# Forming the rests of the first phase's weight blocks with an accumulating DMA

## Chip, cores and metric

One core of a Trainium2 chip runs the whole program. The metric is the device time of one execution in microseconds (us), the median of several runs. The engines named here are PE (TensorE, matmuls; PEld is its weight load), DVE (VectorE), ACT (ScalarE), POOL (GpSimd) and SP (SyncE, which only issues DMAs here). DMAs are issued by SP, ACT or POOL and run on 16 DMA engines that all of them share.

## The reference

One step of a hybrid decoder layer for 512 prompt tokens and 8 single-token samples, T = 520 columns in all. It begins with one wide projection of x and goes on with two recurrent branches, a merge, cross-attention and an MLP:

```python
p = x @ W['w_in'][l]                      # (T, 1024) x (1024, 7424): 58 blocks of 128 columns
p_rw = p[..., :N_SHIFT]                   # r, k, v and the low-rank codes: 26 blocks
o_rw, s_rw_l = _rwkv7_branch(p_rw, p_prev, s_rw[l], l, W)      # 16 heads, delta rule with decay
o_lru, h_l, conv_l = _rglru_branch(p[..., C_U:C_Y], p[..., C_Y:C_GATE], s_conv[l], s_h[l], l, W)
gates = jax.nn.sigmoid(p[..., C_GATE:].reshape(p.shape[:-1] + (2, D_MODEL)) + W['mix_gate_b'][l])
mix = (gates[..., 0, :] * o_rw + gates[..., 1, :] * o_lru) @ W['w_out_mix'][l]
x = _layer_norm(ALPHA * x + mix, W['ln1_g'][l], W['ln1_b'][l])
xa = _mem_attention(x, mem_k[l], mem_v[l], W['xa_wq'][l], W['xa_wo'][l])
x = _layer_norm(ALPHA * x + xa, W['ln2_g'][l], W['ln2_b'][l])
hdn = jnp.square(jax.nn.relu(x @ W['mlp_up'][l]))
x = _layer_norm(ALPHA * x + hdn @ W['mlp_down'][l], W['ln3_g'][l], W['ln3_b'][l])
```

All arrays are float32.

## The kernel before

**Split products.** A float32 product is made of three matmuls in the rounded format F32R: a weight block w is split into a rounded part h = round(w) and a rest l = w - h, x likewise, and `mm3` (L123) adds wh·xh, wh·xl and wl·xh, in this order, for each of the eight 128-row slices of the block. A unit of work is one block of 1024x128 weights: 48 matmuls, half of them over the first 256 columns of x, half over the other 264. So the rest of a block is first read by the third matmul of its unit.

**Units.** `unit` and `wunit` (L149, L152) append to the list `units`; `adv` (L171) runs the next one. Before it runs unit i it calls `prep(i + 1 + AHEAD)` with AHEAD = 2 (L155), and `prep` calls `split_w` (L89) for each block not yet prepared. So a block is loaded and split two units ahead of its use.

**The split (L89 to L99).** SP loads the block into `raw` (tag `wr`, 512 KB in rows of 512 bytes, two buffers), ACT casts it into `h` (tag `wh`, L95), and DVE subtracts: `l = raw - h` (tag `wl`, L98). `wh` and `wl` have three buffers each. The cast of block i+2 therefore waits until the matmuls of unit i-1 have read that buffer for the last time, and the load into a `raw` buffer waits until the subtraction that read it has ended.

**The first phase.** Its 58 units are the blocks of `w_in`: two low-rank codes (`u_code`), 24 of r, k, v (`u_rkv`), 16 of the RG-LRU branch (`u_L`), 16 of the gates (`u_G`). Their epilogues run on ACT and DVE (`shifted`, L441: L445, L446, L447), those of `u_G` on ACT, with stores from POOL (L576). Between the units run the stages of the RWKV-7 branch for four pairs J of head groups: E1, E2, E3 (elementwise, ACT and DVE), C1 (products within a chunk), C2 (a triangular solve of 30 dependent steps on DVE, L718 and L720, with units called in between as filling), the recurrent chain (`stage_chain`, L746: short matmuls with copies on ACT, L771, L806, and on DVE, L778, L794, between them, one step after every 13 to 16 other matmuls) and GN (normalization). After the first phase come the projections of the memory, of the branches, and so on; their blocks go through the same `split_w` or, in the MLP, through `need` (L1641).

**POOL** begins with the loads of the parameter rows (L291), then adds the parts of x and stores them (L1205, L1206; two buffers), and later makes small copies for the outputs (L533, L540, L564), scales `ar` (L678), clears tiles (L682, L714) and issues stores (L566, L576, L851). It takes its instructions in the order of its queue.

**What sets the order.** The program is written for a planner that puts each engine's instructions into an order by the place in the program and by when the inputs should be ready. `keep_in_program_order` pins an instruction behind those already written for its engine. Each engine then runs its own order and waits for semaphores.

Of the kernel before, what the change touches and what calls it, by code (L numbers as in the profile page):

```python
# [8 lines left out]
F32 = mybir.dt.float32  # L9
F32R = mybir.dt.float32r  # L10
AF = mybir.ActivationFunctionType
OP = mybir.AluOpType
# [24 lines left out]
def build(tc, d, dbg=None):  # L37
    nc = tc.nc
    ACT, DVE, POOL, SP = nc.scalar, nc.vector, nc.gpsimd, nc.sync
# [49 lines left out]
    def split_w(src, shape, pool):  # L89
        raws.append(raws.pop(0))  # L90
        raw = raws[-1].tile([128, *shape], F32, tag="wr", name="wr")
        SP.dma_start(out=raw, in_=src)
        h = pool.tile([128, *shape], F32R, tag="wh", name="wh")
        l = pool.tile([128, *shape], F32R, tag="wl", name="wl")
        a = ACT.copy(h, raw)  # L95
        if state["behind"]:
            tc.keep_in_program_order(a)
        DVE.tensor_tensor(l, raw, h.bitcast(F32), op=OP.subtract)  # L98
        return h, l  # L99


# [42 lines left out]

    AHEAD = 2
    units = []
    state = {"prep": 0, "run": 0, "later": [], "x": None, "half": 0, "behind": False}

    def unit(src, fn, shape=(KT, 128), extra=0):  # L149
        units.append([src, fn, shape, extra, None])  # L150
# [4 lines left out]
    def prep(n):  # L155
        while state["prep"] < min(n, len(units)):
            u = units[state["prep"]]
            u[4] = split_w(u[0], u[2], state["x"][u[3] - 1] if u[3] else wsp)
            state["prep"] += 1
# [11 lines left out]
    def adv(n=1):  # L171
        for _ in range(n):
            i = state["run"]
            if i >= len(units):
                return
            prep(i + 1 + AHEAD)
            u = units[i]
            state["run"] += 1
            u[1](u[4])
            u[4] = None  # L180
            flush(False)
# [309 lines left out]
    def u_rkv(q, j):  # L491
        def run(w):
            s, nm = j % 2, "rkv"[q]
            o = et(nm + str(s))
            shifted(mm_full(w, X), q * KT + j, o)
            pair.setdefault(j, {})[nm] = o
        wunit("w_in", q * D + j * 128, run)
# [633 lines left out]
    def u_kv(nm, i):  # L1131
        def run(w):
            p = mmps()[:, 0, 0:N_MEM]
            n = 0
            for k in range(KT):
                c = slice(k % 2 * N_MEM, (k % 2 + 1) * N_MEM)
                for a, b in ((w[0], mem["h"]), (w[0], mem["l"]), (w[1], mem["h"])):
                    PE.matmul(p, a[:, k], b[k // 2][:, c], start=n == 0, stop=n == 3 * KT - 1)
                    n += 1
            ft = (E.tile([128, 2, N_MEM], F32, tag="s1", name="ft", bufs=2) if i % 4 < 2 else  # L1140
                  E.tile([128, 2, N_MEM], F32, tag=("bk", "kp")[i % 2], name="ft"))
            ACT.copy(ft[:, 0], p)  # L1142
            if nm == "xa_wk":
                ACT.dma_start(out=kT_d[i], in_=ft[:, 0])

            def rows():
                pt = ps1()
                for m in range(2):
                    PE.transpose(pt[:, m * 128:(m + 1) * 128], ft[:, 0, m * 128:(m + 1) * 128], ident)
                ACT.copy(ft[:, 1], pt[:, 0:N_MEM])  # L1150
                tok = ft[:, 1].rearrange("p (m n) -> p m n", m=2)
                cs = slice(i * 128, (i + 1) * 128)
                ACT.dma_start(out=d["mem_k_p" if nm == "xa_wk" else "mem_v_p"][0, 0].rearrange(
                    "(m p) h e -> p m (h e)", p=128)[:, :, cs], in_=tok)
                if nm == "xa_wv":
                    ACT.dma_start(out=v_d.rearrange("m p n -> p m n")[:, :, cs], in_=tok)
            later(rows, 2)
        wunit(nm, i * 128, run)
# [16 lines left out]
    C2U = ("kGKGGrv", "GKGkrv", "kKrv")  # L1175
    CHU = ("LLVR", "LLRV", "LLRV")
    FILL = ((3, 4, 8, 18, 20, 21, 22), (3, 7, 9, 16, 28, 31), (3, 13, 23, 28))
    for J in range(3):
        j = 2 * J + 2
        for c in C2U[J] + CHU[J] + "GGG":  # L1180
            if c == "L":
# [4 lines left out]
            else:  # L1186
                u_rkv("rkv".index(c.lower()), 2 * J + 2 + c.isupper())
    CHU = [c.replace("L", "LL") for c in CHU]
    for i in range(KT):
        u_kv("xa_wk", i)  # L1190
    for i in range(4):
# [19 lines left out]
    for J in range(4):  # L1211
# [9 lines left out]
        if J < 3:  # L1221
# [3 lines left out]
            queue(stage_E1(J + 1))  # L1225
            n = len(CHU[J])
            adv(n - (2, 4, 4)[J])
# [620 lines left out]
    def more():  # L1848

        x = ExitStack()  # L1850
        state["x"][1] = x.enter_context(tc.tile_pool(name="wx2", bufs=2, reuse_waits="tile"))
        return x

    adv(KT)
    x = more()
# [29 lines left out]
    x = more()  # L1885
# [103 lines left out]
```

## Time and profile before

| | |
|---|---|
| three runs, us | 1382.88, 1374.3, 1370.4 (median 1374.3) |
| the profiled execution, us | 1374.86 |
| its span, first to last instruction, us | 1373.2 |
| mean granted clock of TensorE | 0.977 |
| busy: PE, DVE, ACT, POOL | 94%, 71%, 46%, 26% of the span |

The profile is of one execution. Its page gives the busy time of each engine, the span in 40 slices of 34.3 us with the busy share in tenths, the queues of the DMAs and the costliest groups of instructions. The trace behind it can be asked for stretches, groups, waits and instructions in order of time. Matmuls overlap, so their durations add up to more than PE's time. "idle before <-X" names what ended the wait before an instruction.

### The profile page before, as it was taken

How to read it: one execution, taken by the hardware profiler on the slowest of the kernel's cores; microseconds unless marked ns; L12 is line 12 of the kernel's file. 1: busy time of each engine (PE TensorE's matmuls, PEld its weight loads, DVE VectorE, ACT ScalarE, POOL GpSimd, SP SyncE). 2: the span in 40 equal slices, each digit the busy share in tenths (PEclk: the TensorE clock that was granted, in tenths of full speed). 3: DMA queues.
4: the chain of work that ended last, by engine and by line, in shares of the span. 5: the costliest groups of instructions: out<-in, count | busy, mean ns of one | idle time of the engine just before them, and what ended most of it. 6: DMA issues, size and time to landing. Idle time of an engine off the chain costs nothing. (4 is left out here: it accounts for less than half of the span.)

```text
span 1373.2 us, 27593 instructions
## 1 busy us (share of the span) xinstructions
PE 1287.6 (94%) x11098; PEld 1195.0 (87%) x11098; DVE 977.0 (71%) x1921; ACT 625.7 (46%) x1202; POOL 356.5 (26%) x415
## 2 busy tenths in 40 slices
PE   7997999999999999878899998989999999999996
PEld 7996998798879787777879998767999999999996
DVE  5578976798669777988954545665668677777755
ACT  4475376437653657542254334432454333333321
POOL 6312000200020012117413133262111444534312
PEclk9999999999999999989999999999999999999998
DMA  6422322231222123475549536684332333333311
GB/s 199 132 78 69 101 66 73 78 101 49 76 91 70 32 80 120 120 204 163 178 140 297 150 107 192 202 262 157 90 102 81 96 91 108 93 93 96 106 64 63
DMA packets 205973, 160.30 MB, mean 117 GB/s; under 512 B 12429, under 2 KB 190911, under 8 KB 205334
## 3 DMA queue, kind: packets, MB, share of 16 engines
q1 hardware_dynamic: 182502, 104.36, 26.0%
q0 software_dynamic: 14592, 47.80, 10.5%
q10 hardware_dynamic: 8752, 6.39, 1.5%
q8 instruction: 87, 1.43, 0.5%
q14 instruction: 40, 0.33, 0.1%
HBM read 137.11 MB, written 21.40 MB: 115 GB/s over the span
## 5 line engine op out<-in xcount | busy, mean ns | idle before, releaser
L47 PE MATMUL mm<-xH,wh 128*128 128x260 f32 (+2 forms) x1824 | 480.9, 292 | 6.3 <-ACT wh L95 2.1
L47 PE MATMUL mm<-xL,wh 128*128 128x256 f32 (+2 forms) x1824 | 473.2, 288 | 1.0 <-DVE ff L1817 1.0
L47 PE MATMUL mm<-xH,wl 128*128 128x264 f32 (+2 forms) x1568 | 453.1, 289 | 0.8 <-DVE wl L98 0.8
L47 PEld LDWEIGHTS mm<-xH,wh 128*128 128x128 f32 x1824 | 329.7, 191 | 16.7 <-issue 3.8
L47 PEld LDWEIGHTS mm<-xL,wh 128*128 128x128 f32 x1824 | 328.7, 190 | 7.8 <-issue 4.5
L47 PEld LDWEIGHTS mm<-xH,wl 128*128 128x128 f32 x1568 | 298.2, 190 | 7.2 <-issue 3.8
L95 ACT CAST wh<-wr 128x1024 fp32r<-128x1024 f32 x120 | 125.1, 1053 | 169.4 <-PE mm L47 127.4
L47 PE MATMUL mm<-hl,wh 128*128 128x260 f32 (+2 forms) x1056 | 197.9, 286 | 1.0 <-ACT hl L1471 0.9
L98 DVE TENSOR_TENSOR wl<-wr,wh 128x1024 fp32r<-128x1024 f32 x120 | 154.4, 1293 | 58.3 <-ACT wh L95 56.7
L47 PEld LDWEIGHTS mm<-hl,wh 128*128 128x128 f32 x1056 | 164.4, 189 | 2.6 <-ACT hl L1471 1.0
L47 PE MATMUL mm<-hl,wl 128*128 128x260 f32 (+2 forms) x528 | 151.1, 286 | 0.0
L1649 DVE TENSOR_TENSOR wl<-wr,wh 128x512 fp32r<-128x512 f32 x104 | 91.6, 887 | 15.0 <-ACT wh L1648 14.6
L47 PEld LDWEIGHTS mm<-hl,wl 128*128 128x128 f32 x528 | 99.9, 189 | 0.6 <-issue 0.5
L1648 ACT CAST wh<-wr 128x512 fp32r<-128x512 f32 x104 | 62.3, 620 | 54.3 <-PE mm L47 37.6
L47 PE MATMUL mm<-xL,wl 128*128 128x260 f32 (+2 forms) x256 | 72.4, 283 | 0.0
L1817 DVE TENSOR_TENSOR ff<-ff,mm 128x520 f32<-128x520 f32 (+2 forms) x64 | 40.0, 625 | 39.8 <-PE mm L47 39.8
L533 POOL COPY OUTC<-ut 128x3 f32<-128x3 f32 x8 | 2.5, 319 | 194.5 <-ACT ut L529 194.5
L1649 DVE TENSOR_TENSOR wl<-ws,wh 128x512 fp32r<-128x512 f32 x48 | 39.1, 817 | 13.3 <-ACT wh L1648 13.1
L47 PEld LDWEIGHTS mm<-xL,wl 128*128 128x128 f32 x256 | 48.2, 188 | 0.0
L47 PE MATMUL mm<-mh,wh 128*128 128x256 f32 x128 | 39.2, 308 | 7.7 <-ACT ft L1142 6.1
L47 PE MATMUL mm<-mh,wl 128*128 128x256 f32 x128 | 38.4, 301 | 4.9 <-DVE wl L98 4.9
L718 DVE TENSOR_TENSOR tmp<-Am,Tm 64x30 f32<-64x30 f32 (+14 forms) x120 | 40.6, 338 | 3.2
(526 smaller groups left out, 2522.7 us busy)
## 6 DMA issues: line engine op xcount, KB each, us to landing
wr<-in_w_in_dram SPq DMA_DIRECT2D x58, 512.0 KB
wr<-in_mlp_up_dram SPq DMA_DIRECT2D x32, 512.0 KB
wr<-in_mlp_down_dram SPq DMA_DIRECT2D x32, 512.0 KB
vc<-in_cache_mem_v_dram POOLq DMA_DIRECT2D x32, 256.0 KB, 7.3
ff<-in_cache_mem_k_dram POOLq DMA_DIRECT2D x32, 256.0 KB, 3.9
gat_d<-gt POOLq DMA_DIRECT2D x16, 260.0 KB, 2.8
wr<-in_xa_wk_dram SPq DMA_DIRECT2D x8, 512.0 KB
wr<-in_xa_wv_dram SPq DMA_DIRECT2D x8, 512.0 KB
```

The lines of the kernel that those rows point to most:

```text
L47: r = nc.tensor.matmul(*a, **k)
L95: a = ACT.copy(h, raw)
L98: DVE.tensor_tensor(l, raw, h.bitcast(F32), op=OP.subtract)
L533: POOL.tensor_copy(COUT[:, 0, :, i], ut[:, S:S + 3])
L718: DVE.tensor_tensor(tv, Am[:, i + 1:32, i:i + 1].to_broadcast([64, n, i]), Tm[:, i:i + 1, 0:i].to_broadcast([64, n, i]), op=OP.mult)
L1648: pin(ACT.copy(h, src))
L1649: pin(DVE.tensor_tensor(l, src, h.bitcast(F32), op=OP.subtract))
L1817: DVE.tensor_tensor(z, z, p, op=OP.add)
```

## The change

`split_w` gets a second way to form the rest, for blocks that are prepared while `state["prep"]` is below `state["dma"]`. That number is set to the length of `units` after the last unit of the first phase, and the first block is prepared only after the whole list has been written, so the new way holds for the 58 blocks of `w_in` and the old one for all others.

In the new way ACT writes the negated rounded block into `l`: `raw` times -1.0, rounded to F32R by the write. Then POOL issues a DMA that reads the block once more from the weight's place in HBM (`src`) and adds it onto `l`: l = -h + w. The cast into `h` stays. The subtraction on DVE falls away for these blocks.

```diff
@@ -95,7 +95,11 @@
         a = ACT.copy(h, raw)
         if state["behind"]:
             tc.keep_in_program_order(a)
-        DVE.tensor_tensor(l, raw, h.bitcast(F32), op=OP.subtract)
+        if state["prep"] < state["dma"]:
+            ACT.activation(l, raw, AF.Copy, scale=-1.0)
+            POOL.dma_start(out=l, in_=src, accum_op=OP.add)
+        else:
+            DVE.tensor_tensor(l, raw, h.bitcast(F32), op=OP.subtract)
         return h, l
@@ -144,7 +148,7 @@
-    state = {"prep": 0, "run": 0, "later": [], "x": None, "half": 0, "behind": False}
+    state = {"prep": 0, "run": 0, "later": [], "x": None, "half": 0, "behind": False, "dma": 0}
@@ -1186,6 +1190,7 @@
     CHU = [c.replace("L", "LL") for c in CHU]
+    state["dma"] = len(units)
     for i in range(KT):
         u_kv("xa_wk", i)
```

## Rows read from the trace of the kernel before

**Rows 1.** The page: busy time by engine, and busy tenths in 40 slices.
```profile
PE 1287.6 (94%) x11098; PEld 1195.0 (87%) x11098; DVE 977.0 (71%) x1921; ACT 625.7 (46%) x1202; POOL 356.5 (26%) x415
...
PE   7997999999999999878899998989999999999996
...
DVE  5578976798669777988954545665668677777755
...
DMA  6422322231222123475549536684332333333311
```

**Rows 2.** Table by stretches: start:end, length, busy us by engine, clock, DMA share, GB/s.
```profile
20.00:515.00 495.00, 476.08 (x4445) 432.44 (x4444) 380.51 (x750) 281.57 (x525) 66.17 (x90) 0.99 0.27 82
128.00:171.00 43.00, 42.33 (x356) 41.33 (x357) 40.85 (x80) 15.91 (x27) 3.17 (x5) 1.00 0.34 102
...
824.00:830.00 6.00, 5.68 (x50) 5.47 (x48) 4.28 (x8) 1.49 (x3) 1.60 (x2) 1.00 0.95 278
```

**Rows 3.** Grouped lines to 521 us: count, busy us, mean ns, idle before.
```profile
L98 DVE TENSOR_TENSOR wl<-wr,wh 128x1024 fp32r<-128x1024 f32 x58 | 72.6, 1254 | 26.0 <-ACT wh L95 25.6
L95 ACT CAST wh<-wr 128x1024 fp32r<-128x1024 f32 x58 | 60.9, 1050 | 97.0 <-PE mm L47 85.5 <-DVE Tm L720 4.1 <-DMA wr<-in_w_in_dram 3.9
```

**Rows 4.** Order of time (start, duration, instruction) around three closely followed blocks.
```profile
29.77 1.05 ACT L95 CAST wh<-wr 128x1024 fp32r<-128x1024 f32 x1 [1.15 <-PE mm L47]
...
42.14 0.28 PE L47 MATMUL mm<-xH,wl 128*128 128x256 f32 x1
...
147.40 1.05 ACT L95 CAST wh<-wr 128x1024 fp32r<-128x1024 f32 x1 [3.91 <-PE mm L47]
147.55 0.28 PE L47 MATMUL mm<-xH,wl 128*128 128x256 f32 x1
148.35 0.68 ACT L445 ACTIVATE mst<-mm,PT 128x512 f32<-128x512 f32 x1
148.93 0.17 ACT L446 COPY OUTC<-mm 128x9 f32<-128x9 f32 x1
150.76 1.21 DVE L98 TENSOR_TENSOR wl<-wr,wh 128x1024 fp32r<-128x1024 f32 x1
159.07 0.28 PE L47 MATMUL mm<-xH,wl 128*128 128x256 f32 x1
...
431.55 1.03 ACT L95 CAST wh<-wr 128x1024 fp32r<-128x1024 f32 x1
...
442.95 0.28 PE L47 MATMUL mm<-xH,wl 128*128 128x256 f32 x1
```

**Rows 5.** DMAs by source (KB each, median us to landing), and one on POOL.
```profile
ff<-in_cache_mem_k_dram POOLq DMA_DIRECT2D x32, 256.0 KB, 3.9
...
KTt<-kT_d POOLq DMA_DIRECT2D x1, 1024.0 KB, 8.9
Vt<-v_d POOLq DMA_DIRECT2D x1, 1024.0 KB, 11.1
...
L1866 POOL DMA_DIRECT2D KTt<-kT_d x1: 902/902/902, 824.3 to 824.3; - x1
```

**Rows 6.** Order of time at the start: first block and POOL's last parameter loads.
```profile
13.94 1.04 ACT L95 CAST wh<-wr 128x1024 fp32r<-128x1024 f32 x1 [3.64 <-DMA wr<-in_w_in_dram]
16.30 0.58 PE L47 MATMUL mm<-xH,wl 128*128 128x256 f32 x1 [0.76 <-DVE wl L98]
17.75 1.05 PE L52 MATMUL ps<-ident,xt 128*128 128x128 f32 x4
17.96 1.61 POOL L291 DMA_DIRECT2D sg<-in_state_lru_conv_dram  x3
```

**Rows 7.** Waits of PE and of POOL to 515 us: total us, times, longest.
```profile
PE ps L52 <- DVE SC L675: 4.7, 3, 1.7
...
POOL OUTC L533 <- ACT ut L529: 194.5, 8, 52.9
...
POOL xf L1205 <- DMA x_d<-xf: 14.0, 6, 4.2
```

## The prediction

> **What bounds the kernel now.** I read the page first, then the table by stretches, then the grouped lines, and last the instructions in order of time where weight blocks follow one another most closely. The page shows PE busy for 94% of the span, in the first phase (slices 1 to 15, up to about 515 us) at nines almost throughout, while DVE stands at five to nine tenths and the DMA engines at two to four [rows 1]. The table says it more sharply: between 20 and 515 us PE works 476.1 of 495.0 us, DVE 380.5, ACT 281.6, POOL 66.2 [rows 2]. So the order of PE's matmuls sets the time of this phase, and what any other engine sheds can return no more than PE's idle time, 495.0 - 476.1 = 18.9 us. The reader should see that a DVE at 77% is busy but is not what ends the phase.
>
> **What the change removes.** 58 subtractions on DVE, 72.6 us in all (1254 ns each) [rows 3]. DVE is off the path that sets the end, so the gain is bounded by 0 and by those 18.9 us. The row nearest to it is the longest of PE's waits on DVE, 4.7 us before the transposes of `bk` (L52, behind L675) [rows 7]. I take -4. In the solve of `stage_C2` DVE will finish earlier, but PE is full of filling units there (42.33 of 43.00 us) [rows 2], so that is hidden: the units only follow the solve instead of running beside it.
>
> **What it adds on ACT.** One more pass over the same 128x1024 block, from `raw` into `l`. The nearest row is the cast of L95, 1050 ns [rows 3]; 58 of them are 60.9 us, and ACT goes from 281.6 to 342.5 of 495 us, 69%. Queued behind each are the epilogues of the unit that has just ended and the copies of the recurrent chain, for which PE waits. Bounds: 0, and half an instruction for every block, 30 us. PE's order leaves other matmuls between two steps of the chain, and DVE hops of the same chain lose an equally long neighbour, so I take +2. `raw` is now freed by ACT's second pass, about when DVE freed it before, so SP's next load moves little.
>
> **What it adds on POOL and the DMA engines.** 58 DMAs of 512 KB, which read the block from HBM a second time and add it onto `l`. No accumulating DMA is in the trace. Issue: POOL held 902 ns for a 1 MB load [rows 5], so about 52 us in all on an engine that works 66 of 495. Time to landing: 256 KB took 3.9 us, 1 MB 8.9, and 1 MB queued behind another 11.1 [rows 5]. Two such transfers together moved 278 GB/s [rows 2]; at that rate 256 KB take 0.9 us, which leaves 3.0 fixed. Lower end, the block counted once: 3.0 + 1.9 = 4.9 us. Upper end: 11.1. I take the addition as moving the block twice (source and old content read): 3.0 + 3.8 = 6.8 us.
>
> The Trainium skill ("DMA: Bandwidth & Descriptors", Anatomy of one DMA) fits a software-issued DMA as about 2.0 us plus bytes over 436 GB/s. By it the block would land after an estimated 3.2 us and the start below would cost 3.6 us less; the row decides, since half as many bytes took 3.9 us.
>
> **Where the new path is covered.** Before, a rest was ready one DVE instruction after its rounded block. Now it needs ACT, POOL and a DMA. Its cover is the two-unit lead: `wh` and `wl` have three buffers, so the cast of block n+2 starts when unit n-1 ends, and its rest is first read by the third matmul of unit n+2. In a close stretch the cast ends at 148.45, the rest came at 151.97, PE read it at 159.07 [rows 4]; units follow every (159.07 - 147.55)/2 = 5.76 us. After the change: the unit's epilogue on ACT ends at 149.10, the negated copy at 150.15, and the DMA lands at 150.15 + 6.8 = 156.95. That is 2.1 us early: hidden. There are 14 blocks with a cover of 10 to 12 us (the first and the last are in [rows 4]: 30.82 to 42.14, 432.58 to 442.95); most others have 13 to 30. With 11.1 us to landing the rest is 2.2 us late; since three buffers go round, a delay d costs d/3 for each close unit: 0.73 x 14 = 10 us.
>
> **POOL's queue.** POOL executes in order. Between 20 and 64 us it waits for its own stores of x, 14.0 us in six waits, the longest 4.2 [rows 7]; a rest queued behind one eats the 2.1 us of spare and 2.1 more. Five close blocks lie there: 0 to 10 us. Most rests stand earlier in the program than these stores: +1.
>
> **The start.** Here there is no cover. The first cast ends at 14.98 and PE reads the first rest at 16.30 [rows 6]. Now the negated copy ends at 16.03 at the earliest, and POOL issues parameter loads until 19.57 [rows 6], all ahead in the program. Issued then, the rest lands at 26.4, 10.1 us late; PE can pull about 1.05 us of transposes into the wait: 9.0. If the planner slips the DMA between the parameter loads: 16.03 + 4.9 = 20.9, and 3.6 us. I take +7, nearer the upper end, since POOL's order mostly follows the program.
>
> **The sum** is made against the profiled execution, 1374.9 us (span 1373.2 and 1.7 around it), 0.6 above the median 1374.3 of the three runs: 1374.9 + 7 (start) - 4 (DVE) + 2 (ACT) + 1 (POOL) = 1381.9, called 1382.
>
> **Rivals.** (a) *The rests come late in the close stretches: slower.* The DMA engines are busy for 0.34 of 43 us while 102 GB/s x 43 us = 4.4 MB pass [rows 2], 3.3 us for 1 MB and 1.75 for a block. Per close unit that is 0.34 x 5.76 = 1.96 us; an addition at twice the price makes it 5.5 of 5.76, at three times 7.2, and then the engines set the pace: 1.45 x 14 = 20 us. It decides from 8.9 us to landing on (150.15 to 159.07). With 11.1 us: +10, and +4 at the start: 1396. With three times the price: about 1407. For it: the block is moved in 512-byte rows and the raw loads share the engines. Against it: at the double price everything still fits.
>
> The Trainium skill ("Collectives: The Full Stack", Part 3, the bandwidth ceiling) says that a reducing DMA reads two sources on one queue and so runs at about half a copy's rate. That speaks for the double price, hence for engines nearly full; no run shown here has such a DMA.
>
> (b) *POOL's queue takes the place of the DVE wait: slower.* POOL waits 194.5 us, at most 52.9 at a time, for the copies of `ut` that end a unit [rows 7]. A rest queued behind such a wait starts after the unit before last instead of earlier, and has one unit plus 0.23 us, 6.0, for 6.8 us and about 0.6 of ACT: 1.4 late. For the eight copies 11 us, with the sixteen gate stores treated alike 34: 1393 to 1416. Against it: the planner places the DMA by when its inputs are ready, and these waits are long because POOL has nothing else to do.
>
> (c) *DVE's relief is worth more: faster.* PE's 18.9 idle us shrink by more than the start costs. If the planner hides the start to 3.6 and 8 to 18 us return: 1361 to 1371. For it: PE waits for DVE where a group of heads begins. Against it: faster by over 1% needs almost all of the idle time, part of which belongs to ACT and to DMA.
>
> **Chances.** Mine (1372 to 1388): 0.52. (a) 0.28, (b) 0.08, (c) 0.12. About 1% (13.7 us) is what a measurement of this kernel can tell from no change. Faster by over 1% is the far end of (c): 0.05. Within 1%: mine nearly whole and the rest of (c): 0.58. Slower: (a), (b) and a little of mine: 0.37. The range for 8 in 10 leaves out most of (c) below and the worst of (a) and (b) above: 1370 to 1415; my own case alone is 1372 to 1388.
>
> **What would show it.** In the profile after: no DVE subtraction on L98 before about 520 us, 58 more passes on ACT, 58 DMAs `wl<-in_w_in` on POOL with a landing of 5 to 9 us; the first unit ending near 31 us instead of 24; then units 5.76 us apart as before in the close stretches, with PE not waiting for `wl`. Landings above 9 us, a DMA share near 0.9 in those stretches, or waits of PE on a DMA `wl` would make (a) right; POOL waiting on ACT just before such a DMA, (b). If the first unit ends at 24 us, the term of the start is wrong.

## The result, and the profile after

The changed kernel takes 1406.6 us (median, 1405.8 to 1411.3), the kernel before 1372.6 beside it: a ratio of 1.0255, 95% interval 1.0216 to 1.0295, so some 35 us more. The forecast was 1382, so its range held the time and its likeliest case (1372 to 1388) did not. The profiled execution took 1405.8 us (span 1404.1), and all lines below are of that one.

Two views of the page first, busy times with the 40 slices, and the queue that POOL's DMAs use (packets, MB, share of 16 engines). First the kernel before, the queue alone:

```profile
q0 software_dynamic: 14592, 47.80, 10.5%
```

Then the changed kernel:

```profile
PE 1297.1 (92%) x11098; PEld 1201.7 (86%) x11098; DVE 912.5 (65%) x1863; ACT 678.9 (48%) x1260; POOL 439.9 (31%) x473
...
PE   5888999999999999888898999999999999999996
...
DVE  5226856566656856798965637466577777767755
...
DMA  9787795569647845655556844586233333333221
...
q0 software_dynamic: 74912, 78.21, 27.8%
```

DVE has shed its work (977.0 us in [rows 1], 912.5 now) and PE shows idle time where it showed none: slice 1 falls from 7 to 5, slices 2 and 3 from nines to eights. The DMA engines, mostly at 2 to 4 tenths in the first phase before, stand at 4 to 9. The 58 blocks pass over them a second time: 78.21 - 47.80 = 30.4 MB.

The table by stretches says where (start:end, length, busy us by engine, clock, DMA share, GB/s). Before, from 20 to 75 us:

```profile
20.00:75.00 55.00, 54.95 (x446) 53.43 (x445) 33.43 (x83) 27.07 (x52) 18.47 (x22) 1.00 0.47 141
```

After, the whole phase and the same stretch:

```profile
20.00:515.00 495.00, 454.27 (x4116) 412.41 (x4116) 299.75 (x635) 309.60 (x538) 140.88 (x136) 0.97 0.73 134
...
20.00:75.00 55.00, 41.55 (x291) 40.01 (x290) 17.61 (x54) 22.02 (x42) 30.08 (x30) 0.94 0.88 179
```

DVE is busy for 81 us less in the same 495 us than in [rows 2]: the subtractions were 72.6, and the delayed stretch also holds less of the program. PE does 21.8 us less. Of that 13.4 lie in the first 55 us. The time went where PE stands, not where DVE was relieved.

**The new operations** (grouped lines to 540 us, then DMAs by source with the median to landing):

```profile
L100 POOL DMA_DIRECT2D wl<-in_w_in_dram x56 | 87.7, 1591 | 211.5 <-ACT wl L99 169.4 <-PE mm L47 37.8 <-ACT y L810 1.8
L99 ACT ACTIVATE wl<-wr 128x1024 fp32r<-128x1024 f32 x56 | 59.7, 1067 | 0.0
...
wl<-in_w_in_dram POOLq DMA_DIRECT2D x58, 512.0 KB, 7.6
...
x_d<-xf POOLq DMA_DIRECT2D x8, 260.0 KB, 5.2
...
lin_d<-ya POOLq DMA_DIRECT2D x8, 256.0 KB, 5.0
```

An accumulating DMA lands 7.6 us after its issue and holds POOL for 1.59 us. The last two lines are stores that the change does not touch. Before they read:

```profile
x_d<-xf POOLq DMA_DIRECT2D x8, 260.0 KB, 2.7
lin_d<-ya POOLq DMA_DIRECT2D x8, 256.0 KB, 2.3
```

**Where the 31 us of the span were lost.** I took the start of each unit's first matmul from both traces and subtracted. The table has the same figure for the experiments that follow, in us against before, at the start of the unit named:

| kernel | unit 1 | 8 | 21 | 28 | 42 | 53 | 57 | end |
|---|---|---|---|---|---|---|---|---|
| the changed kernel | 13.0 | 27.0 | 25.2 | 31.0 | 35.5 | 35.6 | 35.7 | 30.9 |
| only blocks 0 to 2 | 11.9 | 11.1 | 10.0 | 10.0 | 14.4 | 19.1 | 19.1 | 13.2 |
| all but blocks 0 to 2 | 0.2 | 6.8 | 5.2 | 7.7 | 12.3 | 12.3 | 11.7 | 5.2 |
| all but blocks 0 to 8 | -0.8 | -0.7 | -2.2 | 0.5 | 6.7 | 10.5 | 10.3 | 6.0 |
| the same, lin_d's stores by SP | 0.5 | 0.6 | -1.5 | -1.4 | -1.3 | 1.5 | 1.0 | -1.1 |
| x's adds and stores off POOL | 12.0 | 13.5 | 12.1 | 16.6 | 20.8 | 20.8 | 20.0 | 15.2 |
| only the 14 close blocks | -0.3 | -0.2 | -1.5 | -1.5 | -1.7 | -4.8 | -9.9 | -13.4 |
| only blocks 46 to 49 | -0.3 | -0.2 | -0.9 | -0.9 | 0.6 | 3.4 | -1.6 | -6.4 |
| all three places mended | 0.7 | 5.4 | 3.9 | 4.0 | 3.9 | 5.4 | 5.4 | 2.8 |
| before, lin_d's stores by SP | 0.8 | 0.9 | 0.0 | 0.0 | 1.5 | -0.5 | -0.8 | -5.9 |

Between units the order of other matmuls may differ, but at the start of unit 53 each of the kernels whose order I counted had issued the same number since unit 49 (564), and at 57 it is 4724 or 4728 from the start. Each row is one execution, and the three runs of the kernel before alone lie 12 us apart. The last row, a kernel as fast as before, moves by 5 us between unit 57 and the end. So the last column is one execution's, and the timed ratios decide. Read down the first row, the loss has three places: 13 us before unit 1, 14 more in units 4 to 7, and twice some 5 us, near units 27 and 42. Between them the offset stands or falls.

**Place 1, the start.** Order of time (start, duration, engine, instruction, idle before):

```profile
16.67 1.09 ACT L99 ACTIVATE wl<-wr 128x1024 fp32r<-128x1024 f32 x1
...
18.00 1.61 POOL L295 DMA_DIRECT2D sg<-in_state_lru_conv_dram  x3
...
20.46 3.24 POOL L100 DMA_DIRECT2D wl<-in_w_in_dram  x2
...
29.17 0.58 PE L47 MATMUL mm<-xH,wl 128*128 128x256 f32 x1 [5.68 <-DMA wl<-in_w_in_dram]
```

The negated block is ready at 17.76, POOL is through with the parameter loads and four small mask operations at 20.46, and the rest lands at 29.13. PE read the first rest at 16.30 in [rows 6], at 29.17 now: 12.9 us. Into this wait PE pulled the four transposes, further small ones and the first two products of the second unit (16.12 to 23.50), and then stood for 5.68 us. Little was saved by that: the 25 matmuls from 29.17 to 34.50 start 0.21 us apart, against 0.12 from 34.7 on. 0.21 is their distance before at a granted clock of 0.50 (16.30 to 19.30). The table by stretches gives 1.00 for 29.17 to 34.50, which does not fit these distances; in the run with the first three blocks alone the same wait is followed by 0.50, up to 32.7 us.

**Place 2, POOL and its stores of x.** POOL alone:

```profile
50.71 1.34 POOL L1210 TENSOR_TENSOR xf<-xH,xL 128x520 f32<-128x520 f32 x1 [1.88 <-DMA x_d<-xf]
51.99 1.60 POOL L100 DMA_DIRECT2D wl<-in_w_in_dram  x1
...
60.96 1.28 POOL L1210 TENSOR_TENSOR xf<-xH,xL 128x520 f32<-128x520 f32 x1 [4.95 <-DMA x_d<-xf]
62.19 1.61 POOL L100 DMA_DIRECT2D wl<-in_w_in_dram  x1
63.15 1.24 POOL L1211 DMA_DIRECT2D x_d<-xf  x1
69.43 1.31 POOL L1210 TENSOR_TENSOR xf<-xH,xL 128x520 f32<-128x520 f32 x1 [5.04 <-DMA x_d<-xf]
...
72.02 3.24 POOL L100 DMA_DIRECT2D wl<-in_w_in_dram  x2 [0.41 <-issue]
```

POOL waits for a store of x, adds, issues one rest, waits for the next store. The negations of blocks 4, 5 and 6 had ended at 45.41, 51.17 and 56.93, so their DMAs went out 6.6, 11.0 and 15.1 us late, the delay growing from block to block. PE's waits for rests up to 540 us:

```profile
PE mm L47 <- DMA wl<-in_w_in_dram: 15.9, 4, 5.7
```

One of the four is the start's, the other three are these blocks': 10.2 us, and for 10.2 us around them (58.5 to 65.3, 79.0 to 82.4) the granted clock is 0.50. The stores themselves land later, after 5.2 us instead of 2.7. Most are issued behind an accumulating DMA, and the engines are busier (0.88 from 20 to 75 us, before 0.47); these runs do not separate the two.

**Place 3, lin_d's stores.** ACT and POOL around 245 us (before 402 us the same stands again):

```profile
243.98 1.54 POOL L100 DMA_DIRECT2D wl<-in_w_in_dram  x1
244.86 1.25 POOL L570 DMA_DIRECT2D lin_d<-ya  x1
```

```profile
251.76 0.63 ACT L516 ACTIVATE ya<-yb 128x512 f32<-128x512 f32 x1 [3.52 <-DMA lin_d<-ya]
...
252.58 0.69 ACT L449 ACTIVATE mst<-mm,PT 128x512 f32<-128x512 f32 x1
```

```profile
253.37 0.75 DVE L451 SCALAR_TENSOR_TENSOR v<-mm,omu,mst 128x512 f32<-128x512 f32 x1 [0.25 <-ACT OUTC L450]
254.22 2.07 PE L47 MATMUL mm<-xc,bdw 128*128 128x256 f32 x4 [3.18 <-issue]
```

The store is issued right behind an accumulating DMA and lands 6.8 us later. It still reads the buffer `ya`, so ACT stands 3.5 us before the square that writes it, and behind that square, in ACT's order, stands the epilogue (L449) that reads a unit's result from a buffer of `mm`; DVE reads it last (L451). DVE is done with that buffer at 254.12, and PE goes on at 254.22. The profile names no releaser for this wait of 3.2 us ("issue"); the chain is read from the times. PE's granted clock is at 1.2 GHz, the lower of its two levels, for the 6.8 us from 253.1 on (3.4 us at 403.2).

**What held.** A block in a close stretch, ACT, POOL and PE:

```profile
172.56 1.05 ACT L95 CAST wh<-wr 128x1024 fp32r<-128x1024 f32 x1 [3.02 <-PE mm L47]
173.51 0.68 ACT L449 ACTIVATE mst<-mm,PT 128x512 f32<-128x512 f32 x1
...
174.13 1.07 ACT L99 ACTIVATE wl<-wr 128x1024 fp32r<-128x1024 f32 x1
```

```profile
175.50 1.55 POOL L100 DMA_DIRECT2D wl<-in_w_in_dram  x1 [4.11 <-ACT wl L99]
```

```profile
184.23 0.28 PE L47 MATMUL mm<-xH,wl 128*128 128x256 f32 x1
```

The rest lands at 182.80, 1.4 us ahead of its use. The smallest spare in the three close stretches is 0.3 us, the units keep their 5.76 us, and the offset of the changed kernel does not move within them. The table by stretches, around the first of them:

```profile
160.00:195.00 35.00, 35.00 (x294) 35.00 (x293) 27.60 (x67) 18.83 (x28) 11.29 (x10) 1.00 0.97 182
```

The DMA engines are busy for 0.97 of it, and PE works without a break.

### The profile page after: what moved, and what is told of

Its sections match the earlier page's. It is cut to its first block, busy times and chain, and to the rows that moved or that the text cites. A ratio compares the mean times of both kernels' runs of the same rounds, so it can differ in the third digit from the quotient of the medians.

```text
span 1404.1 us, 27657 instructions
## 1 busy us (share of the span) xinstructions
PE 1297.1 (92%) x11098; PEld 1201.7 (86%) x11098; DVE 912.5 (65%) x1863; ACT 678.9 (48%) x1260; POOL 439.9 (31%) x473
## 3 DMA queue, kind: packets, MB, share of 16 engines
q0 software_dynamic: 74912, 78.21, 27.8%
## 5 line engine op out<-in xcount | busy, mean ns | idle before, releaser
L47 PE MATMUL mm<-xL,wh 128*128 128x256 f32 (+2 forms) x1824 | 479.1, 291 | 1.0 <-DVE ff L1822 1.0
L47 PE MATMUL mm<-xH,wl 128*128 128x264 f32 (+2 forms) x1568 | 459.2, 293 | 15.9 <-DMA wl<-in_w_in_dram 15.9
L47 PEld LDWEIGHTS mm<-xH,wh 128*128 128x128 f32 x1824 | 333.8, 193 | 20.1 <-issue 5.0
L47 PEld LDWEIGHTS mm<-xL,wh 128*128 128x128 f32 x1824 | 333.8, 193 | 8.7 <-issue 5.0
L47 PEld LDWEIGHTS mm<-xH,wl 128*128 128x128 f32 x1568 | 303.1, 193 | 23.6 <-DMA wl<-in_w_in_dram 16.6
L100 POOL DMA_DIRECT2D wl<-in_w_in_dram x58 | 90.9, 1590 | 218.7 <-ACT wl L99 176.6
L102 DVE TENSOR_TENSOR wl<-wr,wh 128x1024 fp32r<-128x1024 f32 x62 | 78.8, 1283 | 27.2 <-ACT wh L95 26.9
L99 ACT ACTIVATE wl<-wr 128x1024 fp32r<-128x1024 f32 x58 | 61.8, 1066 | 0.0
L1654 DVE TENSOR_TENSOR wl<-ws,wh 128x512 fp32r<-128x512 f32 x48 | 39.2, 818 | 13.3 <-ACT wh L1653 13.1
```

The costliest lines, as they stand in the source:

```text
L47: r = nc.tensor.matmul(*a, **k)
L99: ACT.activation(l, raw, AF.Copy, scale=-1.0)
L100: POOL.dma_start(out=l, in_=src, accum_op=OP.add)
L1654: pin(DVE.tensor_tensor(l, src, h.bitcast(F32), op=OP.subtract))
```

## The experiments

The first four ask between two theories. Q: the loss is made where something stands in a queue, at the start, at POOL's stores of x, and at lin_d's stores behind an accumulating DMA. T: the loss is the price of 58 second readings and 58 passes of ACT, wherever they lie. In each diff `-` is the changed kernel unless another is named.

**The first three blocks by DVE.**

```diff
-        if state["prep"] < state["dma"]:
+        if 3 <= state["prep"] < state["dma"]:
```

> The first three blocks keep the subtraction on DVE; the other 55 take the accumulating DMA. Theory Q (the loss of 34 us lies in POOL's queue at three places: about 13 us at the start, 14 us at blocks 4 to 6 behind the stores of x, and 4 to 5 us at each of two later places behind the stores of lin_d): the first unit ends near 24 us instead of 37 and the kernel takes about 1394 us. Theory T (the second reading of the weights fills the DMA engines, and the loss is spread over the phase by the amount of traffic): 3 of 58 blocks are 2 us, 1404. Theory A (the second pass on ACT costs it): 1405.

Measured: 1387.4 us, ratio 1.0114 (1.0060 to 1.0168). The first unit ends at 24.4 again, and the 13 us are gone. At units 4 to 7 it now loses 6.8, one gap among them:

```profile
64.81 0.52 PE L47 MATMUL mm<-xH,wl 128*128 128x256 f32 x1 [3.88 <-DMA wl<-in_w_in_dram]
```

That is below the 1394 of Q: the loss at the second place is half as large. POOL has formed and stored two of the eight sums of x (20.41 and 26.00) before its first accumulating DMA, at 29.80. Whether this comes from the three DMAs that are gone or from the units being on time was not separated.

**The first nine blocks by DVE.**

```diff
-        if state["prep"] < state["dma"]:
+        if 9 <= state["prep"] < state["dma"]:
```

> The first nine blocks keep the subtraction on DVE, the other 49 take the accumulating DMA. Theory Q: start and stores of x are free of it, about 27 us return: 1379, with the two losses of 4 to 5 us near 250 and 400 us still there. Theory T: 9 of 58, 5 us return: 1401. Theory A: the same 1401.

Measured: 1380.9 us, ratio 1.0073 (1.0048 to 1.0097), two us over the 1379 expected. With 49 of 58 second readings left, 25 of the 35 us are gone; T gave these nine blocks 9/58 of them, 5 us. Up to unit 25 it even leads before by 2.2 us and loses it again at unit 27 and, above all, at 42.

**The adds and stores of x off POOL.**

```diff
-        POOL.tensor_tensor(t, xH[:, i, :].bitcast(F32), xL[:, i, :].bitcast(F32), op=OP.add)
-        POOL.dma_start(out=x_d[i], in_=t)
+        DVE.tensor_tensor(t, xH[:, i, :].bitcast(F32), xL[:, i, :].bitcast(F32), op=OP.add)
+        SP.dma_start(out=x_d[i], in_=t)
```

> All 58 blocks take the accumulating DMA, but the eight sums for the stores of x are formed by DVE and stored by SP, so POOL has nothing but these DMAs between 20 and 80 us. Theory Q: blocks 4 to 6 land in time, about 14 us return: 1392. Theory T: the same bytes move on the same engines, no change: 1406. If the adds on DVE or the stores on SP's queue get in the way of other work, a few us less return.

Measured: 1395.4 us, ratio 1.0169 (1.0129 to 1.0209), some 12 us under the changed kernel. POOL between 35 and 55 us, all that it does there:

```profile
39.27 1.55 POOL L100 DMA_DIRECT2D wl<-in_w_in_dram  x1 [11.12 <-ACT wl L99]
44.70 1.54 POOL L100 DMA_DIRECT2D wl<-in_w_in_dram  x1 [3.88 <-ACT wl L99]
51.41 1.54 POOL L100 DMA_DIRECT2D wl<-in_w_in_dram  x1 [5.17 <-ACT wl L99]
```

Each DMA now goes out 0.3 us after its negation, and the offset goes from 12.0 at unit 1 to 13.5 at unit 8 instead of 27.0. The second place is POOL's queue. The traffic is all still there.

**ACT's pass alone.** The negation stays, and DVE's subtraction overwrites it; no second reading.

```diff
-            POOL.dma_start(out=l, in_=src, accum_op=OP.add)
+            DVE.tensor_tensor(l, raw, h.bitcast(F32), op=OP.subtract)
```

> The second pass on ACT stays (it writes the negated block into the rest's buffer), but the rest is then formed by the old subtraction on DVE, which overwrites it; there is no second DMA. This prices the ACT pass alone. Theory Q: 0 to 5 us above the kernel before, 1373 to 1378. Theory A: most of the 34 us, 1395 or more. Theory T: as the kernel before, 1373.

Measured: 1381.5 us, ratio 1.0056 (1.0029 to 1.0083), above what Q expected. 5.6 us of it are there when the first unit ends: in ACT's order the negation of block 0 stands before a cast of x and the copies that form `PT`, that of block 1 directly behind its cast. PE waits 1.6 us behind ACT at 19.38 and 1.1 for DVE's subtraction at 21.52. Later DVE's overwriting subtraction has to wait for the negation, a chain that neither kernel has, so the rest of its 8 us says little of ACT's pass in the changed kernel. Of the 13 us at the start some 5 to 6 may thus be ACT's pass; that they add up with the DMA's share was not tried.

**The first nine by DVE, and lin_d's stores by SP** (against the run with nine).

```diff
-                POOL.dma_start(out=lin_d[i], in_=ya)
+                SP.dma_start(out=lin_d[i], in_=ya)
```

> The first nine blocks keep the vector engine's subtraction, as in the run with nine, and the stores of lin_d are issued by SP instead of POOL. Theory Q (what is left of the loss is lin_d's stores standing behind an accumulating DMA on POOL's software queue, which hold the buffer ya): of the 1380.9 of the run with nine, some 3 us at unit 27 and some 6 at unit 42 go; lin_d's landing comes back from 5.0 to under 3 us, TensorE has no gap over 2 us at the gate matmuls near 250 and 400 us that before lacks, and the time is 1372 (1368 to 1376). Theory T (the second reading of the weights and the scalar engine's passes cost time wherever they lie): the stores' queue is not the matter, 1379 to 1383, and the offset still jumps at units 27 and 42.

**The kernel before with that one edit**, as the control:

> The kernel before, with the stores of lin_d issued by SP alone: the control for the run beside it. Theory Q: in the kernel before nothing of weight stands in front of these stores, they land in 2.3 us, so nothing is won: 1372.5 (1370 to 1375). Rival: the stores' own place on POOL's queue costs something before as well, then this is 1364 to 1369 and the gain of the run beside it says nothing of the accumulating DMA; or a store that waits on SP holds back raw blocks, then 1376 or more.

Measured: 1372.3 us, ratio 0.9985 (0.9965 to 1.0006), and for the control 1371.3, ratio 0.9992 (0.9968 to 1.0017). SP's queue takes off 9 us by the medians, 12 by the ratios, with accumulating DMAs and nothing without. What ACT waits for at `ya`, with POOL's stores and nine by DVE:

```profile
ACT ya L516 <- DMA lin_d<-ya: 11.4, 4, 3.7
```

and with SP's:

```profile
ACT ya L516 <- DMA lin_d<-ya: 3.5, 1, 3.5
```

From 360 to 385 us, where unit 42 begins, with POOL's stores and then with SP's:

```profile
360.00:385.00 25.00, 21.64 (x189) 18.84 (x190) 12.82 (x29) 13.19 (x27) 4.54 (x5) 0.86 0.54 99
```

```profile
360.00:385.00 25.00, 24.93 (x260) 21.20 (x258) 16.02 (x38) 15.97 (x32) 5.54 (x5) 1.00 0.66 124
```

PE is full again and the clock with it, although the DMA engines are busier. The third place is the order in POOL's queue of DMAs. With it T falls: 49 second readings and 49 passes of ACT, less what DVE's relief gives back, cost nothing that this measurement can tell. How large the two parts are by themselves it does not say.

**All three places mended**, with 55 of the 58 blocks still by DMA: the condition of the first run, x's edit of the third, lin_d's of the fourth.

> All 55 blocks from the fourth on get their rest by the accumulating DMA; the first three keep the subtraction, the x adds go to the vector engine, and the stores of x_d and lin_d to SP, so that none of the three places of the loss is left. Theory Q: of the 1387.4 of the run with three, some 7 us at units 4 to 8 and some 8 at units 27 and 42 go: 1374 (1370 to 1380), with the first unit's end at 24.4 us and no accumulating DMA of blocks 4 to 6 issued more than 3 us after its negation. Theory T: 55 extra reads of 512 KB and 55 extra passes of the scalar engine are all still there, so at least 1384.

Measured: 1376.1 us, ratio 1.0032 (1.0011 to 1.0054). Of the 35 us 4 are left. They arise before unit 8 (offset 5.4), with one wait of PE for a rest, that of block 3, and in a full stretch:

```profile
38.90 0.58 PE L47 MATMUL mm<-xH,wl 128*128 128x256 f32 x1 [2.35 <-DMA wl<-in_w_in_dram]
```

```profile
20.00:75.00 55.00, 51.88 (x408) 50.80 (x408) 22.25 (x75) 29.93 (x53) 14.57 (x13) 0.96 0.98 199
```

This DMA was issued at 30.25, 0.3 us after its negation, and landed at 38.86: 8.6 us, where the cover of this early block allowed 6.3. Right behind the wait the granted clock is 0.50 for 3.4 us (38.5 to 42.0). Wait and clock, an estimated 2.35 + 3.4/2, make up the 4 us. So a fourth, small place is a landing longer than its cover. Why it took 8.6 us stays open: the engines are full, which would fit T in that one stretch, but they are as full in the close stretch shown above, where nothing is lost.

**A plain second load** in place of the accumulating one, and DVE subtracts in place.

```diff
-            ACT.activation(l, raw, AF.Copy, scale=-1.0)
-            POOL.dma_start(out=l, in_=src, accum_op=OP.add)
+            POOL.dma_start(out=l, in_=src)
+            DVE.tensor_tensor(l, l.bitcast(F32), h.bitcast(F32), op=OP.subtract)
```

> POOL's second DMA only loads the block (no accumulation, no negation by the scalar engine), and the vector engine subtracts the rounded block from it in place, for all 58 blocks. Priced by it: the landing without accumulation, and the second reading without the scalar engine's pass. If the accumulation makes the landing long, the plain DMA lands in 4 to 5 us where the accumulating one took 7.6; if it is the software queue, 7 or more again. The DMA now waits for the free buffer alone, so in the first blocks it need not wait for the rounding; blocks 4 to 6 still stand behind POOL's x adds. Theory Q: first unit's end at 27 to 32 us instead of 37.1, 8 to 14 us lost at units 4 to 8, the vector engine's work back as before: 1388 (1378 to 1400). Theory T with the second reading alone as the price: 1400 or more.

Measured: 1415.0 us, ratio 1.0312 (1.0272 to 1.0353): a miss as far as the time goes. As a price list it serves. The lines that answer to L100 and to the DMA's landing, and the queue:

```profile
L99 POOL DMA_DIRECT2D wl<-in_w_in_dram x58 | 51.8, 894 | 277.4 <-PE mm L47 224.8
...
wl<-in_w_in_dram POOLq DMA_DIRECT2D x58, 512.0 KB, 5.7
...
q0 software_dynamic: 74912, 78.21, 22.2%
```

The same bytes without accumulation land in 5.7 us instead of 7.6 and hold POOL for 0.89 us instead of 1.59. In time of the 16 engines a block costs (22.2% x 1414.0 - 10.5% x 1373.2)/58 = 2.9 us plain and (27.8% x 1404.1 - 144.2)/58 = 4.2 accumulating, 1.45 times as much. The Trainium skill ("Collectives: The Full Stack", Part 3) gives the reducing DMA of a collective half a copy's rate; here it is 1/1.45, so the rule points the right way and is too dear for this pair. The DMA here must wait until PE has left the buffer (224.8 us of POOL's idle time end so), and everything else of POOL's stands behind that wait. The first unit ends at 38.2: its rest's bytes land at 27.28, and PE waits for DVE's subtraction until 30.91. Where the rest of its 43 us goes I did not take apart.

**The start alone.**

```diff
-        if state["prep"] < state["dma"]:
+        if state["prep"] < 3:
```

> Only the first three blocks get their rest by the accumulating DMA, the other 55 as in the kernel before: the start's loss by itself. Theory Q: the first unit ends at 37 us instead of 24, no later block of these three is late, and what is lost at the start is not given back, since TensorE is the bound behind it: 1385 (1381 to 1388). Rival R (the x adds and the work that waits at the start take it up, since TensorE's queue has other work to draw on): the offset falls under 8 us by unit 10, 1380 or less. Theory T (each second reading costs its part of 34 us): three of 58, 1374.

Measured: 1382.4 us, ratio 1.0079 (1.0047 to 1.0112), some 11 us. The offset is 11.9 at unit 1 and 10.0 at unit 28: PE, the bound, gives little back. Here too the later part moves (14.4 at unit 42, 19.1 at 53, 13.2 at the end), although no block there is changed. The step before unit 42 is the clock's: it is 0.50 from 326.2 to 336.5 us. So a single late offset can't be read more closely than some 5 us; the planner's order and the granted clock change with any edit.

**The 14 close blocks alone.**

```diff
-        if state["prep"] < state["dma"]:
+        if state["prep"] in (16,17,18,19,20,31,32,33,34,35,46,47,48,49):
```

> Only the 14 blocks of the three close stretches (16 to 20, 31 to 35, 46 to 49), whose units follow each other in 5.76 us, get their rest by the accumulating DMA. Theory Q: they land just in time (0 to 1.5 us before their first use, 7 to 8 us after their issue), the units keep 5.76 us, nothing is queued behind them that matters: 1372.4 (1370 to 1375). Theory T, and the rival that the close stretches are where the time goes: 14 of 58 of the loss, 1380, or more if a rest comes late by 0.5 us in each block, 1379.

Measured: 1361.7 us, ratio 0.9933 (0.9898 to 0.9968), 9 us faster than before, where Q expected no change and T a loss. DMAs by source:

```profile
wl<-in_w_in_dram POOLq DMA_DIRECT2D x14, 512.0 KB, 7.5
...
x_d<-xf POOLq DMA_DIRECT2D x8, 260.0 KB, 2.7
...
lin_d<-ya POOLq DMA_DIRECT2D x8, 256.0 KB, 2.3
```

The accumulating DMA is as long as ever, and the stores land as fast as before: this choice of blocks, made for another reason, keeps clear of all three places. What is left is a gain, 1.5 us at unit 21, 2.7 at 46 and 9.9 at 57. DVE's relief may be its cause, but 0.9 us at unit 21 also stand in the run with blocks 46 to 49 alone, which has no such DMA by then, and the order changes as well (see the last run). PE does 478.4 us between 20 and 515 us, against 476.1 in [rows 2].

**Blocks 9 to 45, lin_d's stores by SP.**

```diff
-        if 9 <= state["prep"] < state["dma"]:
+        if 9 <= state["prep"] < 46:
```

> The accumulating DMA for the 37 blocks 9 to 45 alone, and lin_d's stores by SP: the version that the run with nine and SP's stores points to, since there the offset against before stood at -2.4 us at unit 46 and rose after it. Theory Q: the offset of -2 to -2.5 us at unit 46 is kept to the end: 1370 (1367 to 1373), at most just faster than before. Theory T: 37 of 58 of the loss are left, 1385 or more.

Measured: 1366.9 us, ratio 0.9982 (0.9957 to 1.0007). The offset is -1.4 us at unit 46 and -1.6 at unit 57, and the ratio can't be told from one. So the first two close stretches, which lie in these blocks, make little of the gain of the 14.

**Blocks 46 to 49 alone.**

```diff
-        if state["prep"] < state["dma"]:
+        if 46 <= state["prep"] < 50:
```

> Only the four blocks 46 to 49 get their rest by the accumulating DMA. The run with all 14 close blocks was faster than before, and against before its TensorE stood at -2.7 us when block 46's unit began and at -9.9 when block 57's did. Theory D (the gain is made behind the third close stretch, where the vector engine no longer has four subtractions between it and the recurrence's work): this kernel stands within 1 us of before up to unit 46, at -5 to -8 at unit 57, and the time is 1364 (1361 to 1368). Rival O (the gain is a chance of the planner's order over the whole phase, which 14 changed blocks gave and four will not): 1370 (1367 to 1374), with no more than 2 us at unit 57.

Measured: 1368.2 us, ratio 0.9958 (0.9937 to 0.9980), some 6 us. That is just outside D's 1361 to 1368 and inside O's 1367 to 1374, and so is the offset at unit 57, -1.6 (D -5 to -8, O at most 2); yet it is a gain. The profile is mixed. From 450 to 475 us in before, with the 14 blocks, and with these four:

```profile
450.00:475.00 25.00, 24.41 (x279) 20.88 (x277) 19.24 (x35) 16.64 (x32) 0.00 (x0) 0.87 0.10 29
```

```profile
450.00:475.00 25.00, 25.00 (x308) 21.12 (x306) 18.80 (x38) 20.27 (x39) 0.19 (x1) 0.93 0.08 23
```

```profile
450.00:475.00 25.00, 24.42 (x253) 18.99 (x254) 15.09 (x25) 12.72 (x24) 0.00 (x0) 0.66 0.08 23
```

The granted clock is 0.66 in this execution, and 26 matmuls fewer than before get through. From unit 53 to 57, with no block by DMA in either, the two kernels gain alike, 5.1 us (-4.8 to -9.9) and 5.0 us (3.4 to -1.6); the run with blocks 9 to 45 gains 0.3 there. Both have the same new order: 198 matmuls between the starts of units 49 and 50, where before, the run with 9 to 45 and the start alone have 60. So four blocks give some 6 of the 9 us. Whether the idle DVE makes it or the order that the planner then writes can't be separated with these runs.

## Why the prediction was right and wrong

That the range held 1406.6 is luck. Its upper part had been added for rivals (a) and (b), and the loss came by neither as they tell it: it came from the start and from POOL's queue, which the forecast had put at 8 us together and which cost some 37.

**The bound: right.** PE sets the time of the phase, and every loss found is a stretch in which PE stands or its clock is low.

**The start: mis-sized, 7 forecast, 11 to 13 measured.** The place and the order were right (first unit late by a rest behind POOL's parameter loads). Three terms were small: POOL was free at 20.46, not 19.57 (mask operations also lie ahead); the landing took 8.7 us, not 6.8, among the raw loads and parameter loads of the start (engines 0.88 busy from 20 to 75 us); and the transposes that were pulled into the wait, counted at 1.05 us, gained little, since PE then ran at the pace of its lower clock until 34.5 us, before only until 19.4. The bound above, 9.0, was built with the middle landing; with the upper one of [rows 5], 11.1, it would have been 13.3 (19.57 + 11.1 - 16.30 - 1.05), and would have held. ACT's pass delays the start as well, which the term left out.

**POOL's queue: the step that failed, 1 forecast, 14 measured.** "Most rests stand earlier in the program than these stores" did not help, since the planner put the adds of x between the DMAs. The 0 to 10 was counted with waits for stores as long as in [rows 7]; but with the DMAs these waits are longer (14.0 us in six, longest 4.2; now 22.2 in five, longest 7.7), and each delayed DMA stands behind the next of them. Whether the same queue or the fuller engines lengthen them is open: with the stores on SP, all three places mended, DVE waits for them up to 7.1 us.

**Missing from the sum: about 10.** I looked at what delays the new DMA on POOL, and not at what the new DMA delays on POOL's queue. lin_d's stores were in the trace, and so were ACT's waits for them: 4.4 us in three before, 10.7 in three now.

**ACT: 2 forecast.** Away from the start no net cost shows: 49 passes, and DVE's relief beside them, stand in a kernel as fast as before.

**Landing and cover: right.** 7.6 us (median; 6.3 to 12.7) for 6.8, and in the close stretches never above 8.2. The spare of 2.1 us shrank to as little as 0.3, and the close stretches kept their pace. Rival (a), late rests in these stretches, had nearly the time (1396 to 1407). Two of its signs are there: the engines are as full as it feared, 0.97 from 160 to 195 us, and PE waits for rests. But these waits lie at the start and in units 4 to 6. The condition that it set for the close stretches, a landing of 8.9 us or more, is not met there, and PE does not wait.

**Rival (b)** named the right engine and the wrong wait. POOL waits less for `ut` (45.5 us, longest 8.4) than in [rows 7], since it now has DMAs to issue; the queue it fears is the one of x and lin_d.

**DVE's relief: -4 forecast.** The row behind it was read generously: the 4.7 us in [rows 7] are three waits together, the longest 1.7. Beside the losses -2 shows in the profile (unit 21, nine by DVE), 0.9 of it also without any such DMA. With no losses a gain of 9 is in the timed runs, from the relief or from the new order: what rival (c) said of a gain may hold for 14 blocks and is false of 58.

**The sum again:** the forecast's own terms add up to 1380.9, not to its 1381.9, which changes nothing in the argument. With what was measured it is 1374.9 + 13 + 14 + 10 - 2 = 1410, for 1405.8; the -4 that remains lies behind unit 57, where one execution differs from another by as much (the control by 5).

## What to carry to other kernels

Before a DMA is put on a queue, list what stands in front of it and also what will stand behind it: a store that still holds a buffer is a wait of whatever writes that buffer next. A detour through a DMA can pay only for blocks whose cover exceeds its landing and whose queue is free at that time: here the kernel with 14 of 58 was 0.7% faster, the one with all 58 2.6% slower. Where the engines are already half busy (0.47 from 20 to 75 us here), bound a landing by the slowest row there is, not by the middle one.

## What the runs showed of the hardware

An accumulating DMA of 512 KB in rows of 512 bytes holds POOL for 1.59 us and lands in 7.6; the plain one holds it for 0.89 and lands in 5.7. A store of 256 KB issued behind the accumulating one lands in 5.0 us instead of 2.3. With the store on another queue ACT's waits for it fall from 11.4 to 3.5 us, while the engines are as busy (0.67 and 0.69 from 20 to 515 us): it is the queue that delays it. In that kernel a second reading of 26 MB (49 blocks of 0.52 MB), less what DVE's relief gives back, cost nothing that could be measured.
